# Twenty weight sums made in DRAM, each begun at its own step of the convolution's and output projections

## The chip, the cores and the metric

One core of a Trainium2 chip. The metric is device time in microseconds (us) of one execution, the median of the runs shown. The engines are TensorE (PE), VectorE (DVE), ScalarE (ACT), GpSimd (POOL) and SyncE (SP); SP, POOL and ACT also issue DMAs, which all run on the same 16 DMA engines.

## The reference

One decoder layer with 512 tokens of width 2048, in float32:

```python
proj = x @ w_in                       # 2048 -> 4352, split into q, k, v, gate_b, gate_c, h
attn = sliding_window_gqa(rope(q), rope(k), v, sinks)       # window 128, 16 heads
conv = gate_b * causal_depthwise_conv(gate_c * h, short_conv_w)
y = concat([attn, conv]) @ w_out                            # 2048 -> 2048
x = layer_norm(2 ** 0.25 * x + y)
u = causal_depthwise_conv(x @ ffn_w_up, ffn_conv_w)         # 2048 -> 11264
a, g = split(u)
y = (silu(a) * g) @ ffn_w_down                              # 5632 -> 2048
out = layer_norm(2 ** 0.25 * x + y)
```

## The kernel before

All weights lie in DRAM as 182 chunks of 128 x 2048 floats (1 MB), in the order of their use: 10 for q, k and v, 24 for the convolution's gates (the conv projection), 16 for the output projection, 88 for the up projection, then the down projection. A chunk is loaded by SP into one of three `raw` buffers (`dma_to`, L161), and is used as two halves. A float32 product is made of three fast ones: `split` (L189) has ACT write the rounded half `whi` and DVE the rest `wlo`, and `mm3` issues three matmuls. A half is 24 matmuls of 512 columns on PE. `whi` and `wlo` have four buffers each, so the split of half j + 4 waits until PE is done with half j. The activations `x` come in eight pieces through `xraw` (`load_x`, L174), each asked for behind a weight chunk and split in the same way into `act`, one piece per half of the first q panel.

The steps in order: q panel 0 (halves 0 to 7), k and v (8 to 11), q panel 1 (12 to 19), the conv projection with the attention between its steps (halves 20 to 67, loop index i = 0 to 47), the output projection (halves 68 on), the first layer norm, then up and down. After each q panel `q_evac` turns its four results by the rotary angles (`rope`): DVE writes `wa` and `wb`, two buffers each, and POOL adds them into `qm` (L268). k does the same into `kr`. The attention of a unit begins with `qs` (L317) on DVE and transposes on PE (L320).

Up and down projections save products by sums of weight blocks (a Winograd form of Strassen's scheme). For the down projection, two such sums per column block are made ahead, wholly in DRAM: 20 of them, (n, p) with n = 0 to 9 and p = 5 or 7. `w_sum` makes one of three DMAs issued by POOL: a copy of a 1 MB chunk into the DRAM tile `sum` (L577), and two 512 KB DMAs that add another chunk's halves to it (L581). The copy reads and writes only DRAM, so it depends on no engine; the additions wait for their copy. The sums are read again in the down projection (L587, L161). In the code the copies and additions stand in the conv loop, a copy at every even step and its additions three steps later (L841).

The order of the instructions on an engine is not that of the code: a list scheduler places an instruction as soon as what it depends on is thought to be ready. POOL's other work is small: rotary additions, the `wq` additions for the up projection (L451), the norm's tables `gb` (L905), and parts of the layer norms.

Of the kernel before, what the change touches and what calls it, by code (L numbers as in the profile page):

```python
# [8 lines left out]
F32 = mybir.dt.float32  # L9
F32R = mybir.dt.float32r  # L10
AF = mybir.ActivationFunctionType
ALU = mybir.AluOpType
# [24 lines left out]
C_OUT = C_CONV + NC_CONV  # L37
# [3 lines left out]
NB = 2 * (NF // 8)  # L41
# [86 lines left out]
class Kernel:  # L128
# [99 lines left out]

    def tok_half(self, j, ks, n, k0, pss, tbs=range(NTB), ahead=2):
        hi, lo = self.half(j, ks, ahead)  # L230
        for k in range(ks):
            kt = k0 + k
            if j == 0 and k == 0:
                ops = ((0, hi), (0, lo), (1, hi))
                for a, (part, ws) in enumerate(ops):
                    for tb in tbs:
                        self.nc.tensor.matmul(pss[tb], self.A(part, 0, slice(tb * P, (tb + 1) * P)), ws[:, 0, :],
                                              start=a == 0, stop=False)
                continue
            for tb in tbs:  # L240
                sl = slice(tb * P, (tb + 1) * P)
                self.mm3(pss[tb][:, :n], self.A(0, kt, sl), self.A(1, kt, sl), hi[:, k, :], lo[:, k, :],
                         kt == 0, kt == KT - 1)
# [322 lines left out]
        c = slice(1024 * h, 1024 * (h + 1))  # L566
        self.nc.gpsimd.dma_start(t[:, c], self.ws_d[C_DOWN + 4 * n + i][:, c], accum_op=ALU.add)

    def w_sum(self, k):

        s = k // 2 if k % 2 == 0 else (k - 3) // 2
        if not 0 <= s < 2 * NB:
            return
        n, p = s // 2, (5, 7)[s % 2]
        w = lambda i: self.ws_d[C_DOWN + 4 * n + i]
        if k % 2 == 0:
            self.nc.gpsimd.dma_start(self.sums[n, p], w(3))  # L577
        else:
            for h in range(2):
                c = slice(1024 * h, 1024 * (h + 1))  # L580
                self.nc.gpsimd.dma_start(self.sums[n, p][:, c], w(0 if p == 5 else 2)[:, c], accum_op=ALU.add)  # L581

    def d_load(self, n):

# [163 lines left out]
    def run(self):  # L748
# [85 lines left out]
        for i in range(2 * NC_CONV):  # L834
            j = 2 * C_CONV + i
            q = i % 4
            if q == 0:
                pss = [self.psum("mm") for _ in range(2)]
            hi, lo = self.half(j, 4)
            self.feat_half(hi, lo, q, pss)  # L840
            self.w_sum(i - 2)  # L841
            if q == 3:
                self.conv_evac(i // 4, pss)
            for u, off in ((i, 0), (i - 1, 1), (i - 4, 2), (i - 5, 3)):
                if u % 2 == 0 and 0 <= u // 2 < 16:
                    n = u // 2
                    if off == 0:
                        st[n] = self.att_q(*units[n])
                    elif off == 1:
                        st[n] = self.att_scores(*units[n], st[n])  # L850
                    elif off == 2:
                        st[n] = self.att_transpose(*units[n], st[n])
                    else:
                        self.att_values(*units[n], st.pop(n))
# [28 lines left out]
        j = 2 * C_OUT  # L883
# [36 lines left out]
        for tb in range(NTB):  # L920
            ps = self.psum("mm")
            sl = slice(tb * P, (tb + 1) * P)
            for kt in range(KT):
                hi, lo = halves[kt // 4]
# [49 lines left out]
        n = len(self.order)  # L974
# [29 lines left out]
        for i, (m, p, h) in enumerate(self.todo[n:]):  # L1004
            self.prepare(n + i + 4)
            u, c = divmod(m, 2)
# [29 lines left out]
            k = end.index((m, p))  # L1036
# [41 lines left out]
```

## Time and profile before

| | us |
|---|---|
| median of 3 runs | 2045.75 (2043.38 to 2046.54) |
| the profiled execution | 2044.12 |
| its span in the trace | 2042.3 |
| PE busy | 1935.0 (95%) |
| DVE busy | 1383.6 (68%) |
| ACT busy | 921.3 (45%) |
| POOL busy | 308.8 (15%) |

In the trace an engine's row says when an instruction began, how long it took, and, in brackets, how long the engine was idle before it and what ended that. A DMA is issued in half a microsecond to a microsecond and lands later; "to landing" is the time between the two. PE's matmuls overlap in the pipeline, so the time of one is read from the distance between starts. The granted clock (PEclk) is a share of full speed, 1.00 being 2.4 GHz.

### The profile page before, as it was taken

The page shows a single profiled execution, that of the slowest core. Times are in us where ns is not written, and L with a number is a line of the kernel's source. Part 1 is how long each engine was busy: PE and PEld are TensorE (multiplying, and loading weights), DVE is VectorE, ACT ScalarE, POOL GpSimd, SP SyncE. Part 2 cuts the span into 40 slices and gives each one's busy share as a digit, 9 for nine tenths or more (in the row PEclk, how much of TensorE's full clock was granted, in tenths as well). Part 3 has the DMA queues.
Part 4 walks back from the last instruction along what each step waited for, and adds up shares of the span by engine and source line. Part 5 has one row for each costly group of instructions (what it writes and reads, how often), then busy time and mean ns, then how long its engine had stood idle before and what let it go on. Part 6 is the DMA issues. An engine that isn't in the chain of part 4 may idle for free. (4 is left out here: it accounts for less than half of the span.)

```text
span 2042.3 us, 26061 instructions
## 1 busy us (share of the span) xinstructions
PE 1935.0 (95%) x9998; PEld 1645.7 (81%) x9998; DVE 1383.6 (68%) x1959; ACT 921.3 (45%) x1403; POOL 308.8 (15%) x361
## 2 busy tenths in 40 slices
PE   7893999999999699999999999999999799999997
PEld 5682888888889588888888888888887588888876
DVE  3332767635334877777777777777777777887887
ACT  2220455433111555555555555555555564454441
POOL 2223000000001511121111111111121001101104
PEclk9896999999999999999999999999999899999999
DMA  9999622154432669999999999999999687877852
GB/s 306 270 295 260 184 78 83 63 165 156 154 103 87 183 155 261 244 261 254 244 262 236 270 254 245 262 242 268 247 249 262 185 235 200 234 225 201 266 193 82
DMA packets 98172, 430.19 MB, mean 211 GB/s; under 512 B 10240, under 2 KB 21536, under 8 KB 72896
## 3 DMA queue, kind: packets, MB, share of 16 engines
q0 software_dynamic: 40928, 174.76, 42.2%
q1 hardware_dynamic: 56544, 252.73, 34.1%
q8 instruction: 78, 1.28, 0.2%
q10 hardware_dynamic: 576, 1.05, 0.1%
q14 instruction: 46, 0.38, 0.1%
HBM read 408.58 MB, written 61.87 MB: 230 GB/s over the span
## 5 line engine op out<-in xcount | busy, mean ns | idle before, releaser
L191 DVE TENSOR_TENSOR wlo<-raw,whi 128x1024 fp32r<-128x1024 f32 (+1 forms) x358 | 437.3, 1223 | 292.8 <-ACT whi L190 292.4
L190 ACT CAST whi<-raw 128x1024 fp32r<-128x1024 f32 (+1 forms) x358 | 373.4, 1045 | 536.3 <-PE mm L222 107.5
L500 PE MATMUL mm<-act,whi 128*128 128x512 f32 x1056 | 379.3, 400 | 8.9 <-DVE act L191 6.7
L502 PE MATMUL mm<-act,wlo 128*128 128x256 f32 x1056 | 297.3, 282 | 0.0
L500 PE MATMUL c<-x,whi 128*128 128x512 f32 x704 | 250.8, 393 | 0.0
L500 PEld LDWEIGHTS mm<-act,whi 128*128 128x128 f32 x1056 | 199.2, 189 | 58.4 <-DVE act L191 7.0
L451 POOL DMA_DIRECT2D wq<-ws x132 | 127.9, 971 | 703.1 <-DVE wlo L191 559.7
L191 DVE TENSOR_TENSOR wlo<-wq,whi 128x1024 fp32r<-128x1024 f32 x132 | 161.3, 1223 | 83.5 <-ACT whi L190 83.3
L502 PEld LDWEIGHTS mm<-act,wlo 128*128 128x128 f32 x1056 | 200.6, 190 | 0.0
L502 PE MATMUL c<-x,wlo 128*128 128x256 f32 x704 | 199.0, 283 | 0.0
L190 ACT CAST whi<-wq 128x1024 fp32r<-128x1024 f32 x132 | 138.5, 1050 | 133.8 <-PE c L500 51.3
L500 PEld LDWEIGHTS c<-x,whi 128*128 128x128 f32 x704 | 132.2, 188 | 30.3
L221 PE MATMUL mm<-act,whi 128*128 128x512 f32 x384 | 152.0, 396 | 0.0
L223 PE MATMUL mm<-act,wlo 128*128 128x512 f32 x384 | 150.4, 392 | 0.0
L222 PE MATMUL mm<-act,whi 128*128 128x512 f32 x384 | 150.1, 391 | 0.0
L221 PE MATMUL mm<-whi,act 128*128 128x512 f32 (+1 forms) x316 | 120.8, 382 | 21.9 <-ACT act L190 20.8
L502 PEld LDWEIGHTS c<-x,wlo 128*128 128x128 f32 x704 | 132.3, 188 | 0.0
L500 PE MATMUL b<-act,whi 128*128 128x512 f32 x352 | 128.5, 404 | 1.5 <-DVE act L191 1.5
L500 PE MATMUL mm<-x,whi 128*128 128x512 f32 x352 | 125.3, 393 | 0.0
L222 PE MATMUL mm<-wlo,act 128*128 128x512 f32 (+1 forms) x316 | 119.6, 378 | 0.3 <-DVE wlo L191 0.3
L223 PE MATMUL mm<-whi,act 128*128 128x512 f32 (+1 forms) x316 | 119.3, 377 | 0.0
L648 PE MATMUL mm<-whi,act 128*128 128x512 f32 x256 | 99.8, 390 | 5.0 <-DVE z L664 3.3
(217 smaller groups left out, 3868.2 us busy)
## 6 DMA issues: line engine op xcount, KB each, us to landing
raw<-ws SPq DMA_DIRECT2D x170, 1024.0 KB, 7.6
wq<-ws POOLq DMA_DIRECT2D x132, 512.0 KB, 9.2
wq<-ws SPq DMA_DIRECT2D x44, 512.0 KB, 8.1
raw<-ws POOLq DMA_DIRECT2D x44, 512.0 KB, 7.2
sum<-ws POOLq DMA_DIRECT2D x40, 512.0 KB, 15.1
wqd<-ws POOLq DMA_DIRECT2D x40, 512.0 KB, 7.2
hd<-ca SPq DMA_DIRECT2D x44, 256.0 KB, 9.6
h<-hd SPq DMA_DIRECT2D x22, 512.0 KB, 5.2
```

The source lines that it names most:

```text
L190: self.nc.scalar.copy(hi, src)
L191: self.nc.vector.tensor_tensor(lo, src, hi.bitcast(F32), op=ALU.subtract)
L221: mm(ps, sh, mh, start=start, stop=False)
L222: mm(ps, sh, ml, start=False, stop=False)
L223: mm(ps, sl, mh, start=False, stop=stop)
L451: self.nc.gpsimd.dma_start(dst, self.ws_d[C_UP + UP_PIECES[2 * f + i]][:, 1024 * j:1024 * (j + 1)], accum_op=ALU.add)
L500: mm(ps, hi[:, sl], x[:, k, :, :].rearrange("p a t -> p (a t)"), start=new and k == 0, stop=False, skip_group_check=not new)
L502: mm(ps[:, :H], lo[:, sl], x[:, k, 0, :], start=False, stop=k == 7, skip_group_check=not new)
L648: mm(ps[b], xh, hi[:, k, :], start=new and h == 0 and k == 0, stop=False, **kw)
```

## The change

`w_sum` gets the step's `lo` half as a second argument. Where it had two kinds of step, it now starts a whole sum at every third step: a DMA of one element from `lo` into the first element of the sum's tile, then the copy, which overwrites that element and must wait for that DMA, then the two additions. The conv loop calls it with i instead of i - 2, which gives sums 0 to 15 (i = 0, 3, ..., 45); `tok_half` calls it in the output projection for the halves 68 on, which gives sums 16 to 19 (halves 68, 71, 74 and 77).

```diff
     def tok_half(self, j, ks, n, k0, pss, tbs=range(NTB), ahead=2):
         hi, lo = self.half(j, ks, ahead)
+        if C_OUT <= j // 2:
+            self.w_sum(j - 2 * C_OUT + 48, lo.rearrange("p a b -> p (a b)").bitcast(F32))
...
-    def w_sum(self, k):
-
-        s = k // 2 if k % 2 == 0 else (k - 3) // 2
-        if not 0 <= s < 2 * NB:
+    def w_sum(self, k, t):
+
+
+        s = k // 3
+        if k % 3 or not 0 <= s < 2 * NB:
             return
         n, p = s // 2, (5, 7)[s % 2]
         w = lambda i: self.ws_d[C_DOWN + 4 * n + i]
-        if k % 2 == 0:
-            self.nc.gpsimd.dma_start(self.sums[n, p], w(3))
-        else:
-            for h in range(2):
-                c = slice(1024 * h, 1024 * (h + 1))
-                self.nc.gpsimd.dma_start(self.sums[n, p][:, c], w(0 if p == 5 else 2)[:, c], accum_op=ALU.add)
+        self.nc.gpsimd.dma_start(self.sums[n, p][0:1, 0:1], t[0:1, 0:1])
+        self.nc.gpsimd.dma_start(self.sums[n, p], w(3))
+        for h in range(2):
+            c = slice(1024 * h, 1024 * (h + 1))
+            self.nc.gpsimd.dma_start(self.sums[n, p][:, c], w(0 if p == 5 else 2)[:, c], accum_op=ALU.add)
...
-            self.w_sum(i - 2)
+            self.w_sum(i, lo.rearrange("p a b -> p (a b)").bitcast(F32))
```

On POOL, at the second q panel's evacuation (L268, `qm`), before; `DMASW` are the semaphores of POOL's own DMAs, so a row that waits for one stands until an earlier DMA has landed:

```order
L577 DMA sum_5_120<-ws 16x16384 [waits DMASW4_49]
L581 DMA sum_7_119<-ws 128x1024 [waits DMASW5_49,DMASW1_49]
L581 DMA sum_7_119<-ws 128x1024
L577 DMA sum_7_121<-ws 16x16384 [waits DMASW7_49]
L581 DMA sum_5_120<-ws 128x1024 [waits DMASW4_49,DMASW0_49]
L581 DMA sum_5_120<-ws 128x1024
L577 DMA sum_5_122<-ws 16x16384 [waits DMASW2_49]
L581 DMA sum_7_121<-ws 128x1024 [waits DMASW7_49,DMASW3_49]
L268 TENSOR_TENSOR qm_189<-wa,wb 128x512 [waits DVE_49]
```

And the same place now (the addition's line is L270, the sums' lines are L579 for the one element, L580 and L583):

```order
L270 TENSOR_TENSOR kr<-wa,wb 128x128 [waits DVE_49] x4
L579 DMA sum_5_106<-wlo 1x1 [waits DVE_49]
L580 DMA sum_5_106<-ws 16x16384 [waits DMASW4_49]
L583 DMA sum_5_106<-ws 128x1024 [waits DMASW5_49]
L583 DMA sum_5_106<-ws 128x1024
L270 TENSOR_TENSOR qm_189<-wa,wb 128x512 [waits DVE_49]
L270 TENSOR_TENSOR qm_190<-wa,wb 128x512 [waits DVE_49]
L270 TENSOR_TENSOR qm_191<-wa,wb 128x512 [waits DVE_49]
L270 TENSOR_TENSOR qm_192<-wa,wb 128x512 [waits DVE_49]
L579 DMA sum_7_107<-wlo 1x1 [waits DMASW0_49,DVE_49]
L580 DMA sum_7_107<-ws 16x16384 [waits DMASW1_49,DMASW0_49]
```

Before, seventeen of the twenty copies stood ahead of this `qm` addition; now one whole sum does, and the other nineteen follow, each behind its own one-element DMA.

On DVE, from the last two results of that evacuation to the first scores of the attention, before:

```order
L191 TENSOR_TENSOR wlo<-raw,whi 128x1024 [waits Activation_49]
L263 TENSOR_TENSOR wa<-mm,rope_t 128x512 [waits Pool_49]
L266 TENSOR_TENSOR wb<-mm,rope_t 128x8x32 [waits DVE_49]
L266 TENSOR_TENSOR wb<-mm,rope_t 128x8x32
L263 TENSOR_TENSOR wa<-mm,rope_t 128x512 [waits PE_49,Pool_49]
L266 TENSOR_TENSOR wb<-mm,rope_t 128x8x32 [waits DVE_49]
L266 TENSOR_TENSOR wb<-mm,rope_t 128x8x32
L317 TENSOR_TENSOR qs<-qm_189,qs 128x4x64 [waits Activation_49]
L191 TENSOR_TENSOR wlo<-raw,whi 128x1024 [waits DMAHW2_49,PE_49,Activation_49]
L317 TENSOR_TENSOR qs<-qm_189,qs 128x4x64 [waits PE_49,Activation_49]
```

And now:

```order
L265 TENSOR_TENSOR wa<-mm,rope_t 128x512 [waits PE_49,Pool_49]
L268 TENSOR_TENSOR wb<-mm,rope_t 128x8x32 [waits DVE_49]
L268 TENSOR_TENSOR wb<-mm,rope_t 128x8x32
L265 TENSOR_TENSOR wa<-mm,rope_t 128x512 [waits PE_49,Pool_49]
L268 TENSOR_TENSOR wb<-mm,rope_t 128x8x32 [waits DVE_49]
L268 TENSOR_TENSOR wb<-mm,rope_t 128x8x32
L319 TENSOR_TENSOR qs<-qm_189,qs 128x4x64 [waits Activation_49]
L191 TENSOR_TENSOR wlo<-raw,whi 128x1024
L191 TENSOR_TENSOR wlo<-raw,whi 128x1024 [waits DMAHW2_49,PE_49,Activation_49]
L319 TENSOR_TENSOR qs<-qm_189,qs 128x4x64 [waits PE_49,Activation_49]
```

One `wlo` has moved behind the evacuation, and the next `wlo` waits for the first one-element DMA (`DMASW4`), since it writes the buffer which that DMA reads. Every third `wlo` after it waits likewise. PE's and SP's order is the same in both kernels.

## Rows read from the trace of the kernel before

**Rows 1.** The page's slices of the span, 40 of 51 us each, in tenths.

```profile
PE   7893999999999699999999999999999799999997
DMA  9999622154432669999999999999999687877852
```

**Rows 2.** Table by stage: stretch, length; PE, PEld, DVE, ACT, POOL busy; PEclk, DMA share, GB/s.

```profile
10.90:84.47 73.57, 51.38 (x182) 38.92 (x181) 21.59 (x27) 16.90 (x23) 11.33 (x16) 0.84 0.98 300
84.47:152.30 67.83, 67.83 (x399) 60.05 (x397) 25.66 (x50) 16.72 (x27) 22.50 (x29) 1.00 0.98 272
152.30:158.30 6.00, 5.92 (x29) 4.61 (x27) 1.91 (x4) 2.11 (x4) 0.39 (x1) 1.00 1.11 311
158.30:191.40 33.10, 0.00 (x0) 0.00 (x0) 5.28 (x8) 0.78 (x1) 13.14 (x16) 0.53 1.02 257
191.40:496.50 305.10, 305.07 (x1492) 255.96 (x1493) 190.03 (x368) 132.03 (x305) 10.26 (x13) 0.99 0.39 118
```

**Rows 3.** PE's waits, whole span: total us, times, longest.

```profile
PE aux L320 <- DVE qs L317: 33.2, 1, 33.2
PE mm L221 <- ACT act L190: 20.8, 5, 6.4
```

**Rows 4.** Timeline of PE in the first panel: start, duration, instruction, idle before.

```profile
10.90 0.39 PE L221 MATMUL mm<-whi,act 128*128 128x512 f32 x1
...
16.11 0.39 PE L223 MATMUL mm<-whi,act 128*128 128x512 f32 x1
...
40.44 0.80 PE L221 MATMUL mm<-whi,act 128*128 128x512 f32 x1 [6.42 <-ACT act L190]
...
44.38 0.39 PE L221 MATMUL mm<-whi,act 128*128 128x512 f32 x1
```

**Rows 5.** ACT's waits in the first 100 us.

```profile
ACT act L190 <- DMA xraw<-xt: 39.6, 9, 10.6
```

**Rows 6.** DMA issues, count, KB, median to landing: first 100 us, then 240 to 420.

```profile
raw<-ws SPq DMA_DIRECT2D x8, 1024.0 KB, 26.3
...
raw<-ws SPq DMA_DIRECT2D x14, 1024.0 KB, 4.8
```

**Rows 7.** Table by stage, in the output projection, while SP loads the residual.

```profile
501.00:517.00 16.00, 16.00 (x72) 13.25 (x71) 3.68 (x3) 3.15 (x3) 0.00 (x0) 1.00 1.01 407
```

**Rows 8.** Timeline of DVE around the second q panel's evacuation.

```profile
136.01 1.23 DVE L191 TENSOR_TENSOR wlo<-raw,whi 128x1024 fp32r<-128x1024 f32 x1 [4.17 <-ACT whi L190]
...
150.98 0.75 DVE L266 TENSOR_TENSOR wb<-mm,rope_t 128x256 f32<-128x256 f32 x2
...
186.12 0.69 DVE L263 TENSOR_TENSOR wa<-mm,rope_t 128x512 f32<-128x512 f32 x1 [31.41 <-POOL qm L268]
```

**Rows 9.** Timeline of POOL at the same place.

```profile
175.97 1.64 POOL L581 DMA_DIRECT2D sum<-ws  x2 [6.22 <-DMA sum<-ws]
...
184.00 0.80 POOL L581 DMA_DIRECT2D sum<-ws  x1 [5.88 <-DMA sum<-ws]
184.55 2.75 POOL L268 TENSOR_TENSOR qm<-wa,wb 128x512 f32<-128x512 f32 x2
```

**Rows 10.** Landing: POOL's stores, a small load, all copies; last, copies issued before 10 us.

```profile
zd<-z POOLq DMA_DIRECT2D x8, 512.0 KB, 3.0
...
scw<-scw POOLq DMA_DIRECT2D x1, 12.0 KB, 6.5
...
sum<-ws POOLq DMA_DIRECT2D x20, 18.3
...
L577 POOL DMA_DIRECT2D sum<-ws x2: 510/516/522, 5.2 to 5.7; - x2
...
DMA to landing us min/median/max: 8.7/9.8/10.9
```

**Rows 11.** From 191.4 us, sums beside the conv projection: stage, POOL's issues, weight loads.

```profile
191.40:222.00 30.60, 30.57 (x145) 25.66 (x146) 15.93 (x33) 12.35 (x31) 7.28 (x10) 0.95 1.03 265
...
L581 POOL DMA_DIRECT2D sum<-ws x8 | 6.6, 956 | 23.6 <-DMA sum<-ws 23.6
...
raw<-ws SPq DMA_DIRECT2D x2, 1024.0 KB, 12.4
```

**Rows 12.** POOL's DMA issues in the up projection, 760 to 1540 us: busy, mean ns.

```profile
L451 POOL DMA_DIRECT2D wq<-ws x119 | 116.2, 977 | 438.0 <-DVE wlo L191 324.5 <-DMA wq<-ws 100.4 <-issue 11.9
```

## Prediction

> **What bounds the kernel now.** I read the slices of the span first. TensorE (PE) is busy in nine tenths or more of nearly every slice; the gaps that matter here lie in the first 200 us, where the DMA row stands at 9 in every slice [rows 1]. The table by stage sizes them: the first q panel holds 51.38 us of PE work in 73.57, k/v and the second q panel run full, and then 33.10 us hold no PE work at all, with the DMA engines at 0.98 to 1.02 throughout [rows 2]. From 191.4 us on PE is full again, at a DMA share of 0.39. PE's waits name two things: one wait of 33.2 us for `qs`, and five waits, 20.8 us together, for the splits of `x` [rows 3]. Those splits wait in turn for the loads of `xraw`: ACT lost 39.6 us to them in the first 100 us [rows 5]. So the start is bound by the DMA engines, and the weight sums are what fills them: a 1 MB weight load takes a median of 26.3 us to land there, and 4.8 us later, when no sums run [rows 6]. The 33 us wait is another matter: at 150.98 us VectorE (DVE) had made the first `wb`, but its third `wa` came only at 186.12, after 31.41 us of waiting for a `qm` addition on POOL [rows 8], and POOL began that addition at 184.55, since the sums' additions stood before it in its queue, each waiting for a copy in DRAM [rows 9]. Both gaps have one cause: nothing in the sums depends on the computation, so the list scheduler put them at the front of POOL's queue.
>
> **What the change does to it.** Each sum now starts with a DMA of one element from the `wlo` tile of its step, which the copy must wait for. The order shows that this takes: all 20 sums now stand behind the four `kr` additions, the first one just ahead of the second panel's `qm` additions; PE's and SP's order is the same, and DVE's and ACT's differ by a few rows around the two q evacuations and the k/v one.
>
> **The first panel.** What PE needs when nothing is late: 23 steps from 10.90 to 16.11 us are 5.21 us, 0.2265 us a matmul [rows 4]. From 10.90 to the panel's end at 84.47 there are 180 matmuls, 40.8 us, against 73.57: an excess of 32.8 us, of which 22 are waits and the rest the lower clock after each (in 40.44 to 44.38 nine matmuls took 3.94 us instead of 2.04, so a wait costs about 1.9 us more than itself) [rows 4]. Are the loads alone fast enough? What must arrive for the last half is six weight chunks of 1 MB, 4 MB of `x` and 0.65 MB of tables, 10.65 MB. With only plain loads in flight the engines moved 407 GB/s later on [rows 7]; that gives 26 us, and even the 300 GB/s of the disturbed stretch [rows 2] gives 35.5, against 46.2 us at which PE can reach the last half (10.90 plus 156 matmuls). So PE becomes the bound. I take 1 us for a late first `x` piece, a gain of **31.8 us**. Bounds: 32.8 above; below, the speed of one load at a time, 1 MB in 4.8 us or 218 GB/s [rows 6], gives 49 us, about 52 with the start and 54 with the split, 8 us late, so 24. I am near the upper end because the prefetch keeps several loads in flight.
>
> **The wait of 33.2 us.** The `qm` additions now stand behind one sum, not behind the rest of twenty. Its chain on POOL, c: one-element DMA, copy, two additions' issues. The trace of before has no such small store; nearest are a 512 KB store from POOL, 3.0 us to landing, and a 12 KB load into the full queues, 6.5 us. The first two copies landed in 9.8 us at the median, all twenty in 18.3 [rows 10]. So c is 0.55 + 3.0 + 9.8 + 1.64 = 15 us (the issues from [rows 9]), and between 15 and 27; I take 15, since without sums ahead of it the queue is no fuller than at the very start, where the 9.8 was taken. The trigger is `wlo` of half 20, written at 136.01 + 1.23 = 137.24 us [rows 8], 15 us ahead of the panel's end at 152.3. POOL would be free at 152.2 and begin the `qm` addition there instead of at 184.55. In before PE resumed at 191.4, 6.9 us after that addition began; so it resumes at 159.1, and the half that covers this ends at 158.3 [rows 2]: a wait of 0.9 us is left. The gain is 33.2 - 0.9 + 1.9 for the clock, **34.2 us**; at c = 27 the addition starts at 164.2, the wait left is 12.8, and the gain about 20.
>
> **The sums in their new place.** They do not vanish: 20 copies and 40 additions now run beside the conv and output projections, with 20 more one-element DMAs. Three covers. First, the DMA engines have room (0.39 busy [rows 2]), and in 191.4 to 222 us the last sums ran beside the conv projection already: share 1.03, weight loads at 12.4 us, and PE busy 30.57 of 30.60 us [rows 11]. A chunk is asked for some seven halves (5.44 us or more each), about 40 us, before its use, so 12.4 us cost nothing. Second, the new wait: `wlo` of half j + 4 may be written only after the one-element DMA has read half j's tile, and behind that write on DVE stand the attention's operations, on which PE depends. POOL has four halves, 4 x 24 x 0.2265 = 22 us, before this bites. Third, POOL must keep pace: 47 halves in the 305.1 us [rows 2] are 6.49 us each, so from half 20 to half 77 there are 48 x 6.49 + 9 x 5.44 = 360 us for 19 chains, 18.97 us each, against c = 15. I put this at **nothing**. Behind the sums on POOL stand three `wq` additions and the two `gb` loads, which come a few steps later than before; both are first needed after the normalisation, and nobody waits for them. The sums themselves are read in the down projection.
>
> The one-element DMA is also priced by a page: the Trainium skill, "DMA: Bandwidth & Descriptors", section on the anatomy of one DMA, gives about 2.0 us fixed plus bytes over 436 GB/s. By it, as an estimate, the small DMA takes 2 us and the copy 4.4, c would be near 9 and the wait left nothing, 1 us better than the sum here; no run here shows it.
>
> **The sum.** 31.8 + 34.2 = 66.0 us. The profiled execution took 2044.12 us (span 2042.3), within 2 us of the median of 2045.75: 1978 by its own time, 1980 against the median.
>
> **Rivals.**
> *The loads alone are too slow*: the first panel gains only 24; 1988. For it: chunks wait for free buffers, three of them. Against: 407 GB/s with plain loads [rows 7].
> *POOL is held by the first sum* (c = 27): 31.8 + 20 are gained; 1994. For it: the median copy took 18.3 us. Against: that median is of copies that queued behind other sums.
> *POOL cannot keep pace* (the other side). If c exceeds 18.97 us by d, 19 d - 22 us are lost, because DVE then stands at a `wlo` until the small DMA has landed. The gain is eaten at d = 88 / 19 = 4.6, that is c = 23.6; at c = 27 the loss is 131 us and the time 2111. For it: c = 27 is what the worst rows add up to. Against: that needs the full queues of the start, and the stretch that they move into stands at 0.39.
> *POOL's DMA issues stretch beside a busy DVE.* Four issues a sum would have to grow from 0.96 to 3.1 us for c = 23.6, and the time would be 2046. Against: beside a DVE busy 15.93 of 30.6 us the issues took 956 ns [rows 11], and in the up projection 977 ns [rows 12]. This is the rule that speaks against the change: the Trainium skill, "SBUF — State Buffer", section "A bandwidth-pool intuition that's wrong", says a POOL-issued DMA of some 620 ns takes about 3100 beside a DVE copy that holds the shared port. By that rule the issues would come out at that break-even; the trace does not bear it out for the DVE operations here.
> *The sums are not held back*: 2046. Only if the small DMA landed at once and out of step; the order speaks against it, since the DMA waits for DVE's `wlo`.
>
> **How the numbers follow.** Forecast 0.80; slow loads 0.06; held POOL 0.06; no pace 0.06 (0.02 of it with c between 20 and 23.6, still faster, 0.04 slower); stretched issues 0.01; not held back 0.01. The time is the forecast's, 1980. At the lower end stand both excesses gone whole, 32.8 + 35.1, less 2 us for the scatter of the runs: 1975. The upper end takes in the two faster rivals with 2 us of scatter: 1996. A measurement of this kernel can tell about 0.2% (4 us) from no change. Faster: 0.80 + 0.06 + 0.06 + 0.02 = 0.94; same 0.02; slower 0.04.
>
> **What the profile after would show.** Right: the k/v panel starts near 53 us instead of 84.5, with PE waiting for `x` no more than a few us; no PE wait for `qs` above 2 us; `sum` DMAs spread evenly from about 105 to 465 us, some 19 us apart; from the output projection on the same durations. Wrong: DVE `wlo` waiting for the DMA of `sum`, growing from sum to sum (no pace); a `qm` addition on POOL waiting behind a copy while PE stands (held POOL); ACT still waiting for `xraw` with no sum in flight (slow loads).

## The result and the profile after

The median went from 2045.31 us (2043.38 to 2046.54) to **1977.39 us** (1974.71 to 1980.19): a ratio of 0.9669, 95% interval 0.9651 to 0.9687. That is 67.9 us less, 2.6 us under the forecast of 1980 and inside its range of 1975 to 1996. The profiled execution of after took 1980.19 us (span 1978.4), the longest of its four.

In the page's slices of after (40 of 49 us), the rows that answer to [rows 1], PE's gap of slices 2 to 4 is gone. The gaps that remain, the first of them in slice 13, stood in before as well.

```profile
PE   9999999999997899999999999999997999999997
DMA  6267766888425699999999999999997787787952
```

The table by stage answers to [rows 2], with the same columns. Its stretches are the rest of the first q panel, k/v with the second panel, the half that covers the evacuation, the conv projection with the attention, and the output projection:

```profile
9.29:50.06 40.77, 40.77 (x181) 33.77 (x180) 22.82 (x30) 17.91 (x25) 0.40 (x1) 1.00 0.67 264
50.06:117.90 67.84, 67.84 (x399) 60.05 (x397) 24.52 (x50) 16.73 (x27) 11.77 (x13) 1.00 0.39 123
117.90:123.90 6.00, 6.00 (x33) 4.98 (x31) 5.84 (x11) 2.11 (x4) 4.79 (x4) 1.00 0.11 21
123.90:427.30 303.40, 303.40 (x1491) 254.54 (x1490) 190.26 (x369) 132.63 (x306) 45.17 (x65) 1.00 0.74 200
427.30:585.80 158.50, 158.50 (x813) 136.16 (x812) 53.76 (x64) 30.52 (x30) 11.05 (x16) 1.00 0.57 185
```

PE's busy time equals the stretch in all five, at a clock of 1.00, and there is no row for the 33.10 us without PE work any more. The DMA work has moved down the table: the share falls from 0.98 to 0.67 in the first panel and rises from 0.39 to 0.74 beside the conv projection.

PE's timeline shows where the time was gained (columns as in [rows 4]). The first is the `L221` that stood at 10.90 in before; the next begins k/v, the third is the `qs` transpose, and the last the scores.

```profile
9.26 0.39 PE L221 MATMUL mm<-whi,act 128*128 128x512 f32 x1
...
50.06 0.28 PE L221 MATMUL aux<-whi,act 128*128 128x256 f32 x1
...
123.66 0.45 PE L322 MATMUL aux<-identr,qs 128*128 128x128 f32 x4
...
129.48 1.12 PE L337 MATMUL aux<-kst,qt 128*128 128x256 f32 x8
```

The last two, in the timeline of before:

```profile
191.43 0.75 PE L320 MATMUL aux<-identr,qs 128*128 128x128 f32 x4 [33.21 <-DVE qs L317]
...
198.68 1.12 PE L335 MATMUL aux<-kst,qt 128*128 128x256 f32 x8
```

k/v begins 84.47 - 50.06 = 34.41 us earlier, the transpose 67.77, the scores 69.20. So the start and the first panel gave 34.4 us, the wait 33.4, and the lower clock behind that wait 1.4 (granted 0.52 from 191.43 to 194.59, where a matmul shows 0.63 us instead of 0.39). Of the 34.4 us, 1.6 lie ahead of the `L221` (10.90 before, 9.26 now) and are no work of the change, as the section on the prediction shows. The first matmul of the up projection keeps this: 685.61 us before, 616.47 after, 69.1 earlier.

PE's two largest waits over the whole span are now these, both behind 616 us; the waits for `qs` and for `x` in the first panel [rows 3] have no row left:

```profile
PE mm L502 <- DVE act L191: 6.3, 1, 6.3
PE b L437 <- DVE x L191: 5.9, 1, 5.9
```

ACT's wait for `xraw` (first 70 us) answers to [rows 5], the landing of the 1 MB loads (first 100 us) to [rows 6]: 39.6 us became 6.2, and 26.3 us became 5.0.

```profile
ACT act L190 <- DMA xraw<-xt: 6.2, 7, 2.2
```

```profile
raw<-ws SPq DMA_DIRECT2D x11, 1024.0 KB, 5.0
```

At the second q panel's evacuation POOL's timeline shows the first sum (L579 the one-element DMA, L580 the copy, L583 the additions), the `qm` additions, and the second sum:

```profile
103.12 0.54 POOL L579 DMA_DIRECT2D sum<-wlo  x1 [24.24 <-DVE wlo L191]
105.01 0.51 POOL L580 DMA_DIRECT2D sum<-ws  x1 [1.34 <-DMA sum<-wlo]
110.36 1.77 POOL L583 DMA_DIRECT2D sum<-ws  x2 [4.85 <-DMA sum<-ws]
117.40 2.56 POOL L270 TENSOR_TENSOR qm<-wa,wb 128x512 f32<-128x512 f32 x2 [5.27 <-DVE wb L268]
...
124.28 0.56 POOL L579 DMA_DIRECT2D sum<-wlo  x1 [1.38 <-DVE wlo L191]
```

POOL waited for DVE there, not for a copy as in [rows 9]: the first sum's last issue was over at 112.13 us, 5 us before the first addition. On DVE the third `wa`, which stood 31.41 us in [rows 8], now stands 0.16, and `qs` follows at 121.27:

```profile
118.74 0.69 DVE L265 TENSOR_TENSOR wa<-mm,rope_t 128x512 f32<-128x512 f32 x1 [0.16 <-POOL qm L270]
...
121.27 0.48 DVE L319 TENSOR_TENSOR qs<-qm,qs 128x256 fp32r<-128x256 f32 x1
```

The sums run from 103.12 to 477.77 us, 19.7 us apart on average. DVE's waits up to 640 us hold one of the signs that the prediction lists under "Wrong":

```profile
DVE wlo L191 <- DMA sum<-wlo: 19.7, 2, 10.3
```

Both come at the very end, for sums 18 and 19 of 0 to 19, and PE did not stand there (the last row of the stage table).

### The profile page after: what moved, and what is told of

Read it like the earlier page. It is cut to its first block, busy times and chain, and to the rows that moved or that the text cites. A ratio compares the mean times of both kernels' runs of the same rounds, so it can differ in the third digit from the quotient of the medians.

```text
span 1978.4 us, 26104 instructions
## 1 busy us (share of the span) xinstructions
PE 1924.8 (97%) x9998; PEld 1641.1 (83%) x9998; DVE 1381.7 (70%) x1959; ACT 920.7 (47%) x1403; POOL 322.2 (16%) x381
## 5 line engine op out<-in xcount | busy, mean ns | idle before, releaser
L221 PE MATMUL mm<-act,whi 128*128 128x512 f32 x384 | 151.5, 394 | 0.0
L221 PE MATMUL mm<-whi,act 128*128 128x512 f32 (+1 forms) x316 | 116.5, 369 | 0.0
L223 PE MATMUL mm<-whi,act 128*128 128x512 f32 (+1 forms) x316 | 116.2, 368 | 0.0
```

Source lines behind the costliest of these rows:

```text
L221: mm(ps, sh, mh, start=start, stop=False)
L223: mm(ps, sl, mh, start=False, stop=stop)
```

## The experiments

The first four ran beside 2045.21 us of before, the last two on another chip, beside 2043.60.

### After, unchanged, once more

> The changed kernel once more, for a second trace and more times. Theory: PE has no gap until the first layer norm (k/v panel at 50.1 us, as in the first trace), so all gain lies ahead of it, and the 5 us between its runs (1975 to 1980) come from the clock after the short waits in the down projection: a run near 1975 shows a granted clock of 1.00 where the first trace shows 0.96 (the 40 us behind the wait that ended at 1550.5, and behind the one that ended at 1915.7). Rival: the runs differ in the first 600 us, through the sums' queue, and then the first matmul of the up projection does not come at 616.5 us in both.

1977.54 us (1974.99 to 1978.08), ratio 0.9669 [0.9654, 0.9683]. The first up-projection matmul starts at 616.50 here and at 616.47 in the first trace, and yet the spans are 1976.3 and 1978.4. So what sets these two traces apart arises behind 616 us. In the first trace, the 69.1 us gained had shrunk to 63.9 at the end. Two stretches of 40 us there, each behind one of PE's waits in the down projection, in the columns of [rows 2]:

```profile
1550.47:1590.47 40.00, 40.00 (x168) 32.73 (x169) 28.01 (x27) 23.00 (x27) 3.97 (x5) 0.96 0.71 199
1915.70:1955.70 40.00, 40.00 (x168) 32.76 (x169) 26.20 (x40) 5.13 (x8) 13.25 (x10) 0.96 0.13 50
```

The same two in this run, and the first of them in before:

```profile
1550.47:1590.47 40.00, 40.00 (x176) 32.91 (x176) 29.55 (x28) 23.57 (x27) 3.98 (x5) 1.00 0.77 213
1912.99:1952.99 40.00, 40.00 (x168) 32.72 (x169) 26.19 (x40) 5.15 (x8) 13.26 (x10) 0.96 0.13 50
```

```profile
1618.33:1658.33 40.00, 40.00 (x175) 32.92 (x176) 29.37 (x29) 23.64 (x27) 3.98 (x5) 1.00 0.72 206
```

The first trace has 168 matmuls in a stretch that holds 175 in before, at a clock of 0.96 against 1.00; there a wait of 2.6 us ended at 1550.47, and 1.68 us in before. This run keeps the 1.00 at that place and loses elsewhere: one of its waits, for `x`, is 8.3 us, where the first trace has 2.2 and 4.6 around the same place.

The expectation holds in part: the run profiled here was not one near 1975 but took 1978.08, and behind the later wait its clock is 0.96 as in the first trace. Nor does the length of a wait alone decide the clock: before has 1.00 over the 40 us behind its wait of 3.30 us at 1981.43, the kernel without the sums (below) 0.96 behind one of 3.16 us at 1910.27. So these traces differ in waits that fall out longer or shorter from run to run, and in the clock behind them. Nothing ties the waits to the sums: at the place of the 8.3 us before has 5.1 and 3.6 us, the kernel without the sums 4.9 and 3.6. Why a wait falls out longer in one run, and what decides the clock behind it, is open.

### The `qm` additions on DVE, the sums as before

```diff
-    def rope(self, dst, ps, nh, tb, which):
+    def rope(self, dst, ps, nh, tb, which, on=None):
...
-        nc.gpsimd.tensor_tensor(dst, t1, t2, op=ALU.add)
+        (on or nc.gpsimd).tensor_tensor(dst, t1, t2, op=ALU.add)
...
-            self.rope(dst, pss[tb], 8, tb, 0)
+            self.rope(dst, pss[tb], 8, tb, 0, self.nc.vector if half else None)
```

> The kernel before, its sums still at the front of POOL's queue, but the second q panel's four rotary additions made by DVE instead of POOL. Theory (two separate losses): the 33 us wait for qs goes, the first panel's loss stays (k/v panel at 84.5 us): 2045.3 - 34.8 + 1 for the longer DVE path = 2011 to 2014. Rival (one loss, full DMA engines hold everything back): PE finds its next wait within the conv projection's first steps and the time stays above 2030.

2007.74 us (2007.07 to 2009.45), ratio 0.982 [0.9804, 0.9837]. PE's largest wait is now the one for `x`, and the first panel is still slow at a full DMA share:

```profile
PE mm L221 <- ACT act L190: 15.9, 5, 4.4
```

```profile
6.00:82.51 76.51, 57.44 (x192) 42.99 (x193) 25.45 (x34) 19.51 (x28) 11.50 (x17) 0.84 1.02 322
```

The `qs` wait is gone with all 20 sums still in their old place. The first panel takes 73.24 us from its first `L221` (9.27) to k/v (82.51), where it took 73.57 in before: it is not mended. k/v begins 1.96 us earlier, nearly all of it from the earlier start, so of the 37.5 us gained about 35.5 are the wait's, against 34.8 in after. The time lies below the 2011 to 2014 expected, since the 1 us put down for a longer DVE path was not needed and the start gave 1.6 in the profiled run. The two losses are separate, and the second one needs POOL's queue: off that queue, the same additions wait for nothing.

### All 20 sums begun behind k/v, ahead of the second q panel

```diff
         self.kv_evac(pss)
+        for s in range(2 * NB):
+            self.w_sum(3 * s, self.vv.rearrange("p t g a d -> p (t g a d)").bitcast(F32)[:, (NTB - 1) * 256:])
         pss = [self.psum("mm") for _ in range(NTB)]
...
-            self.w_sum(i, lo.rearrange("p a b -> p (a b)").bitcast(F32))
```

(The call in `tok_half` goes too.)

> The changed kernel, but all twenty sums begin at the k/v evacuation (the one-element DMAs read the finished v tile), so none runs beside the first panel, and 18 of them stand ahead of the second panel's qm additions on POOL. Theory: the first panel keeps its gain (k/v panel at 50 us) and the wait for qs comes back, as long as 18 sums at 9 to 10 us from about 75 us on, so until about 245 us instead of 124: 2090 to 2110, slower than before. Rival (the wait was due to full DMA engines, not to the order on POOL): a wait of 33 us or less, 2012 or less.

2100.88 us (2100.73 to 2101.03), ratio 1.0275 [1.0254, 1.0295]: slower than before. k/v still begins at 50.05, so the first panel keeps its gain. Then PE waits once, for a result tile that DVE has not read out yet: DVE's third `wa` itself waits 109.8 us for POOL's `qm`. On POOL the first `qm` addition (L268 in this kernel) starts at 258.08, behind the sums' one-element DMAs (L577 here), copies (L578) and additions (L581):

```profile
PE mm L221 <- DVE wb L266: 118.5, 1, 118.5
```

```profile
253.67 1.71 POOL L581 DMA_DIRECT2D sum<-ws  x2 [13.71 <-DMA sum<-ws]
...
257.01 1.65 POOL L577 DMA_DIRECT2D sum<-vv  x2
258.08 3.09 POOL L268 TENSOR_TENSOR qm<-wa,wb 128x512 f32<-128x512 f32 x2
```

So to hold the sums back from the start is not enough. The wait is as long as the sums that stand ahead of `qm` in POOL's queue need; here that is eighteen of them, in after one. This is the rival "POOL is held", made on purpose and larger.

### After, without the sums' 80 DMAs

```diff
-        self.nc.gpsimd.dma_start(self.sums[n, p][0:1, 0:1], t[0:1, 0:1])
-        self.nc.gpsimd.dma_start(self.sums[n, p], w(3))
-        for h in range(2):
-            c = slice(1024 * h, 1024 * (h + 1))
-            self.nc.gpsimd.dma_start(self.sums[n, p][:, c], w(0 if p == 5 else 2)[:, c], accum_op=ALU.add)
...
-            self.nc.gpsimd.dma_start(t, self.sums[n, 5])
+            self.nc.gpsimd.dma_start(t, self.ws_d[C_DOWN + 4 * n + 3])
```

(and the same reading of the plain chunk for `sums[n, 7]`)

> The changed kernel without the sums: their 80 DMAs are left out and the down projection reads the plain weight chunk in their place, so that part of the weights is not what the reference wants; all else is unchanged. Theory: the spread sums cost PE nothing, so the same as the changed kernel within 2 us (1975 to 1980), with the first matmul of the up projection at 616 us. Rival: the sums beside the projections still cost, and this is 5 us or more faster.

1975.43 us (1974.57 to 1976.92), ratio 0.9662 [0.9647, 0.9676]: 2 us under after, with intervals that overlap. The first up-projection matmul starts at 616.46, as in after. Beside the conv projection, first here and then in after:

```profile
118.00:427.00 309.00, 309.00 (x1519) 259.18 (x1517) 195.61 (x378) 134.76 (x309) 7.41 (x7) 1.00 0.28 94
```

```profile
118.00:427.00 309.00, 309.00 (x1518) 259.19 (x1517) 195.70 (x378) 134.44 (x309) 49.86 (x69) 1.00 0.72 196
```

The sums take 0.44 of the DMA engines' time and 42 us of POOL, and not one matmul's time from PE. The prediction's "nothing" is thus measured ahead of the up projection, and there is nothing left there for another placing of the sums to win.

### A sum at every second half instead of every third

```diff
-        s = k // 3
-        if k % 3 or not 0 <= s < 2 * NB:
+        s = k // 2
+        if k % 2 or not 0 <= s < 2 * NB:
```

> The changed kernel with a sum at every second step instead of every third: all 20 in the conv projection, 12.98 us apart instead of 18.97. It tests the rival that POOL cannot keep pace. Theory A: the one-element DMA lands behind the additions of the sum before it, in the same software queue, so a chain that starts right after the last one takes 18.5 us, as the trace after shows in the output projection (397.46, 415.99, 434.19 us): 19 x (18.5 - 12.98) = 105 us, less 22 us until DVE stands and some 18 us until PE runs out of halves: 65 us lost, 2025 to 2060. Theory B: c is 15 us, as in the prediction: 19 x 2 - 22 = 16 us or less, at most 1993.

2010.99 us (2009.33 to 2012.64), ratio 0.9838 [0.9809, 0.9866]: half of the gain is lost. Waits of PE and of DVE up to 640 us, and the stage from 120 to 420 us:

```profile
PE aux L378 <- DVE pt L191: 21.4, 9, 4.6
```

```profile
DVE wlo L191 <- DMA sum<-wlo: 79.2, 10, 14.8
```

```profile
120.00:420.00 300.00, 278.58 (x1337) 231.24 (x1337) 169.71 (x345) 118.78 (x286) 54.66 (x76) 0.97 0.75 200
```

This is the mechanism of "POOL cannot keep pace": DVE stands at `wlo` for the one-element DMA, the attention's operations stand behind it on DVE, and PE behind those. The first up-projection matmul comes at 650.51, 34.0 us later than in after. PE's waits are 21.4 of that, slower matmuls 6.8 (0.2084 us each in this stretch, 278.58 over 1337, where after has 300.00 over 1476), and the slow start of this trace, shown below, 1.8; the other 4 were not traced. The chains follow each other in 16.65 us on average ((417.54 - 134.43) / 17), where two halves give 2 x 6.49 = 12.98. Neither theory held: A had the chain at 18.5 us and the time at 2025 or more, B had 1993 at most. By the prediction's formula, with the measured pace, 19 x 3.67 - 22 = 48 us are lost; 33.5 were measured. The formula is too dear, since it books DVE's waiting to PE us for us, and here DVE waited 79.2 us for these DMAs and PE 21.4. The DMA share of 0.75 is near the 0.72 of after in the same stretch, which speaks against full engines as the reason; the next run tests it.

### The same, with the one-element DMA issued by ACT

```diff
-        self.nc.gpsimd.dma_start(self.sums[n, p][0:1, 0:1], t[0:1, 0:1])
+        self.nc.scalar.dma_start(self.sums[n, p][0:1, 0:1], t[0:1, 0:1])
```

> The same with the one-element DMA issued by ACT, whose hardware queue holds nothing else there. Theory A (the small DMA waits behind the additions in POOL's queue): the chain falls to about 2 + 5 + 2 = 9 us, POOL keeps pace at 12.98 us, and the time is that of the changed kernel, 1975 to 1985. Rival (the DMA engines are too full for a sum every 12.98 us, whatever the queue): still above 2020.

1976.88 us (1976.45 to 1977.32), ratio 0.9671 [0.9643, 0.9699]: the loss is gone, and so are DVE's waits for the sums. The DMA engines are busier than in the kernel above, and PE is full:

```profile
120.00:420.00 300.00, 300.00 (x1476) 251.68 (x1475) 187.16 (x366) 127.70 (x298) 48.66 (x63) 1.00 0.82 225
```

So the rival, engines too full for this pace, falls. The sums themselves are still behind the 12.98 us of two halves: 13.95 us a sum ((365.76 - 142.56) / 16) instead of 16.65, where the theory had POOL's chain at about 9. The landing times say why (issues from 120 to 420 us: count, KB where known, median us to landing; first the kernel above, then this one):

```profile
sum<-ws POOLq DMA_DIRECT2D x18, 5.1
sum<-wlo POOLq DMA_DIRECT2D x18, 0.0 KB, 9.4
```

```profile
sum<-ws POOLq DMA_DIRECT2D x18, 12.9
```

Whichever DMA stands first behind the additions in POOL's own queue lands late: the small one at 9.4 us with the copy at 5.1, or the copy at 12.9. Late copies do no harm here, since only the small DMA holds a `wlo` buffer. So the price of too tight a pace is the held buffer, not the sums' work.

## Why the prediction held, step by step

**The first panel: right, 31.8 forecast, 34.4 measured, which is above the upper bound of 32.8.** The excess that the ledger counted came back whole, 32.8: 40.8 us from 9.26 to 50.06 for 180 matmuls. So the 1 us for a late first piece of `x` was not needed. The other 1.6 us are luck. They lie ahead of the ledger's 10.90 us, in the first twelve matmuls, which stood some 0.4 us apart in the trace of before and some 0.24 in that of after. The sums did not do that, since it does not follow their place: the same `L221`, first in the kernel with `qm` on DVE, which has all its sums at the front, then in the one with a sum at every second half, which has none there:

```profile
9.27 0.39 PE L221 MATMUL mm<-whi,act 128*128 128x512 f32 x1
```

```profile
11.07 0.39 PE L221 MATMUL mm<-whi,act 128*128 128x512 f32 x1
```

The granted clock reads 1.00 in both traces there (6.20 to 10.90 and 6.20 to 9.26), so these rows do not explain it; why some runs start slowly, and how many of the unprofiled ones did, is open. Against the ledger's own stretch the bound of 32.8 held.

**The wait of 33.2: right, 34.2 forecast, 34.8 measured.** The wait left was put at 0.9 us and there is none; the clock behind the wait was put at 1.9 and gave back 1.4. The reason for the first is c, the first sum's chain: 9.0 us (103.12 to 112.13) where 15 was forecast, so POOL was free 5 us before DVE had the first `wb`.

**c itself: mis-sized, and not one number.** Forecast 15 with bounds of 15 and 27. For sums 0 to 12 the chains took 8.8 to 14.8 us, 11.1 on average; the lower bound was too high. The copy took 5.1 us at the median, not 9.8: that price was taken at the very start, in a stretch with a DMA share of 0.98 [rows 2, 10]. For sums 13 to 19 the chains took 16 to 23 us. POOL's timeline from sum 13 on, with the start of sum 19 last, and the landing of the one-element DMAs (100 to 340 us, then 360 to 480):

```profile
362.99 0.54 POOL L579 DMA_DIRECT2D sum<-wlo  x1 [9.52 <-DVE wlo L191]
...
371.31 0.89 POOL L453 DMA_DIRECT2D wq<-ws  x1 [2.51 <-issue]
376.30 0.86 POOL L453 DMA_DIRECT2D wq<-ws  x1 [4.11 <-DMA wq<-ws]
377.37 1.67 POOL L583 DMA_DIRECT2D sum<-ws  x2 [0.21 <-issue]
380.23 0.54 POOL L579 DMA_DIRECT2D sum<-wlo  x1 [1.19 <-DVE wlo L191]
391.08 0.52 POOL L580 DMA_DIRECT2D sum<-ws  x1 [10.30 <-DMA sum<-wlo]
...
477.77 1.12 POOL L579 DMA_DIRECT2D sum<-wlo  x1
```

```profile
DMA to landing us min/median/max: 1.6/4.7/5.7
```

```profile
DMA to landing us min/median/max: 5.0/10.6/14.3
```

For sums 4 to 13 POOL stood 7.4 to 12.2 us idle ahead of each sum (for sums 1 to 3 it was 1.4 to 3.7). Then the last two of three `wq` additions fell between copy and additions of sum 13, whose chain took 16.1 us, and 1.2 us of idle time were left ahead of sum 14. From there on each small DMA was issued right behind the last sum's additions and landed behind them, up to 14.3 us later, so a chain took 18 to 23 us. I had read these `wq` and `gb` issues as work that nobody waits for; they also push what stands behind them. That they started the lateness is read from the trace and was not tried apart; that a DMA behind additions lands late, the two kernels with a sum at every second half show.

The other half of this step is the pace. The prediction set c against a mean of 18.97 us a sum, but the halves that begin the last sums follow faster. DVE's `wlo` that begins sum 13, and the one that begins sum 19:

```profile
361.47 1.23 DVE L191 TENSOR_TENSOR wlo<-raw,whi 128x1024 fp32r<-128x1024 f32 x1 [0.16 <-ACT whi L190]
...
460.54 1.23 DVE L191 TENSOR_TENSOR wlo<-raw,whi 128x1024 fp32r<-128x1024 f32 x1 [4.22 <-ACT whi L190]
```

That is 16.5 us a sum on average. Chains of 18 to 23 us do not fit in it, so the lateness grew: sum 13 began 0.3 us after its `wlo` was written (362.70), sum 19 16.0 us after (461.77 to 477.77). A mean over two stretches with different paces hid that.

By the page that was set against this, c near 9 (the Trainium skill, "DMA: Bandwidth & Descriptors", anatomy of one DMA), the trace agrees for a DMA with nothing ahead of it: 1.6 us for the small one, 4.8 at the least for the copy, 9.0 for the first chain. Behind additions it does not. Beside a weight load the small one is slower too: it took 1.6 us for sum 8, with no load issued from 260 to 263 us, and 4.8 for sum 9, beside a load of 1 MB issued between 281 and 284.

**The sums in their new place at nothing: right**, and measured by taking them out (0.01 us at the first up-projection matmul; 2 us in the median, with intervals that overlap). The second cover, four halves before a held `wlo` bites, was needed at sums 18 and 19 and was enough.

**The sum: 66.0 forecast, 69.2 at the scores in the two traces, 1.6 of it the start.** The other 1.6 us are the 1.0 and 0.6 by which the two gains were put too low. The median shows 67.9; the runs scatter by 5 us.

**The rivals.** *The loads alone are too slow* falls: 5.0 us a load, DMA share 0.67, PE without a gap. *POOL is held by the first sum* falls for this change, and its mechanism is real (all sums begun behind k/v: 118.5 us of wait). *POOL cannot keep pace* falls as a verdict, though it was nearer than its 0.06: its sign showed at the end of after (9.4 us for sum 18, 10.3 for sum 19), and one step closer in the sums' spacing makes it real. *POOL's issues stretch* falls: the additions' issues took these times (min, median, max ns) beside a DVE that was busy 190 of 303 us:

```profile
L583 POOL DMA_DIRECT2D sum<-ws x40: 827/966/1259, 110.4 to 496.1; - x40
```

That is 966 ns against 956 and 977 in [rows 11, 12]; what the Trainium skill, "SBUF — State Buffer", section "A bandwidth-pool intuition that's wrong", tells of a POOL-issued DMA beside a DVE copy, some 3100 ns, does not show beside these DVE operations. *The sums are not held back* falls: the first starts at 103.12 us.

## What to carry to other kernels

Work that depends on nothing is put first by a list scheduler, and on an in-order queue it then stands ahead of work that the path needs: look for an addition that waits behind a DMA of which it reads nothing. A made-up dependency (here one element) spreads such work at no cost as long as each piece ends within its own step; take that step where it is shortest, not as a mean, count everything else on that queue into it, and let the marker DMA go by a queue in which nothing slow stands ahead of it, since until it lands it holds the buffer it reads. Take the price of an operation from a stretch as busy as the one it will run in. Before a gain is put down to a change, look in the other runs whether it follows the change: 1.6 us here did not.

## What the runs showed of the hardware

A DMA of one element in POOL's queue landed in 1.6 us with nothing ahead of it, in 4.8 beside a weight load of 1 MB, and in up to 14.3 us behind two accumulating DMAs of 512 KB; a copy of 1 MB in DRAM took 5.1 us at the median, and 12.9 where it stood first behind the additions. The same one-element DMA issued by ACT instead of POOL turned 79.2 us of DVE's waits into none. Four DMAs a sum cost PE nothing beside its loads, at a DMA share of 0.72 with a sum at every third half and of 0.82 with one at every second. And behind a wait of PE the granted clock over the next 40 us was 1.00 after 1.68 us and 0.96 after 2.6, but also 1.00 after 3.30 and 0.96 after 3.16: the length of the wait alone does not decide it.
